# One load moved from the sync queue to GpSimd's queue in a cosine-similarity attention kernel, with new orders for the first pairs

## The chip, the cores and the metric

The kernel runs on one core of one Trainium2 chip. The metric is the device time of one execution in microseconds (us), taken as the median of several runs. Durations inside the kernel come from one further execution that was recorded by the hardware profiler; times inside it count from the start of its span. The engines are named as the profile names them: PE (TensorE), PEld (its weight load), DVE (VectorE), ACT (ScalarE), POOL (GpSimd) and SP (SyncE, which here only issues transfers). SPq, ACTq and POOLq are the instruction queues from which these engines issue DMAs.

## The reference

For each of 8 x 12 heads, Q, K and V are 512 x 64 in float32. The rows of Q and K are scaled to length one, their products are divided by tau = 0.1, a softmax runs over the keys, and the weights multiply V.

```python
Q_norm = Q / (np.linalg.norm(Q, axis=-1, keepdims=True) + 1e-10)
K_norm = K / (np.linalg.norm(K, axis=-1, keepdims=True) + 1e-10)
scores = np.einsum('bhqd,bhkd->bhqk', Q_norm, K_norm) / tau
weights = np.exp(scores - np.max(scores, axis=-1, keepdims=True))
weights = weights / (np.sum(weights, axis=-1, keepdims=True) + 1e-10)
return np.einsum('bhqk,bhkd->bhqd', weights, V).astype(np.float32)
```

## The kernel before

**Tiling.** Two heads of one batch make a *pair*; there are 48 pairs, numbered s = 0 to 47. A tensor of a pair is 256 KB and lies in SBUF as 128 partitions x 2 heads x 256 numbers. In the names below, w is 0 for Q and 1 for K, h is the head in the pair, and c counts four chunks of 128 keys.

**Operations of a pair**, with the names that the kernel gives them:

- LD(s,w) loads Q or K (L311; pair 0 is loaded by halves, one head each, at L308), LV(s) loads V (L314), ST(s) stores the output (L565).
- SQ(s,w) squares (L329 on ACT, L331 and L337 on POOL; pair 0: L239 on ACT, L241 on POOL). SSQ(s,w) lets PE add eight columns of the squares into one by matmuls with the identity (L354), and RED(s,w) sums what is left on DVE (L361; straight from the squares at L365).
- LOG and NEW(s,7) make the inverse norms of pairs 0 to 3 on ACT (L248, L252, L379, L382). From the fourth group of pairs on NEW is a chain of small DVE steps (L389, L390, L394, L398).
- SCL(s,w) multiplies by the inverse norms and rounds to bf16 (L420 on DVE or POOL, pair 0 at L258), TR(s,w) transposes on PE (L426; pair 0 at L266, L268) and EVA(s) copies the transposes of Q and K out of PSUM on DVE (L434; pair 0 at L279).
- SCO(s,c) makes the scores of a chunk on PE for both heads (L508), EXP(s,c) takes their exponential on ACT (L531; in pair 0 the first two chunks go head by head), VC(s) rounds V to bf16 on POOL (L536), PV(s,h,i) multiplies weights and V on PE (L548), and RCP and NRM divide by the row sums on DVE (L559, L561).

**What sets the order.** Nothing is decided at run time. Each engine has a fixed list of operation numbers, `ORDER` (L644), written out in the kernel, and executes it from front to back; a negative number is a filler matmul of that many columns. Before an operation the engine waits for the semaphores of the operations in its `needs`, so that a waiting operation also holds all that stands behind it in its list. Dependences are recorded by `Program.add` and turned into waits in `Program.run`. A DMA goes to the queue of the engine in whose list it stands and counts up a semaphore of its own buffer; loads of pairs 1 to 3 have one each (`first1_1` for K of pair 1).

**The first lists, in these names.** SP: LD(0,0) head 0, head 1, LD(1,0), LD(1,1), LD(2,0), LD(2,1), LV(0), LD(3,0), LD(3,1), LV(1) and so on. ACT issues the halves of LD(0,1), then: SQ(0,0) for both heads, LOG and NRMS of pair 0, SQ(1,0), a last NRMS, SQ(1,1) of head 0, SQ(2,0), EXP(0,1) of head 0, LOG(1), NEW(1), three more half EXPs of pair 0, LOG(2), EXP(0,2), NEW(2), EXP(0,3), EXP(1,0), LOG(3), EXP(1,1), NEW(3) and from there on EXP alone. POOL: four constants (`eps`, `one`, `eye`, `vone`), SQ(0,1) for both heads, SCL(0,1) for both heads, SQ(1,1) of head 1, SQ(2,1), VC(0), SQ(3,0), SQ(3,1), VC(1), SQ(4,0), SQ(5,0), VC(2), VC(3). PE: eight warm-up matmuls and fillers, TR(0,1) and TR(0,0) of head 0, a filler, SSQ(1,0), TR(0,1) of head 1, a filler, SCO(0,1) of head 0, SSQ(1,1), TR(0,0) of head 1, SCO(0,0) of head 0, and so on.

The ring of Q and K buffers is 15 pairs deep and that of V buffers 10 (`RINGS`, L622), so that none of the first loads waits for a buffer.

Of the kernel before, what the change touches and what calls it, by code (L numbers as in the profile page):

```python
# [108 lines left out]
def bass_cosine_similarity_attention_kernel(  # L109
# [15 lines left out]
    R_QK, R_V, R_SQ, R_QN, R_QT, R_ET, R_O, R_X = RINGS  # L125
# [31 lines left out]
    P = Program(nc)  # L157
# [19 lines left out]
    def key(name, s, *rest):  # L177
        return (name, s) + rest if s >= 0 else None
# [10 lines left out]
    def warm(e):  # L189
        for k in range(WARM):  # L190
            last = e.matmul(out=o_ps[1][:, :], lhsT=ident[:, :], rhs=warm_in[:, :], start=True, stop=True)
        return last
# [97 lines left out]
    def squares(s, w):  # L290
        return [("SQ", s, w if s in SQ_ON else 0)] + ([("SQ", s, w, 1)] if s in SQ_ON and isinstance(SQ_ON[s][w], tuple) else [])
# [5 lines left out]
    def pair(s):  # L297
# [6 lines left out]
        for w, x in ((0, Q), (1, K)):  # L304
            if s == 0:
                for h in range(2):
                    P.add(("LD", 0, w, h), "act" if w else "sp", "ldh", -1000 + h,  [],
                          lambda e, w=w, x=x, h=h: e.dma_start(out=qk[iq][:, w, h], in_=src(x, s)[:, h]), slot=f"head{w}_{h}")  # L308
                continue
            P.add(("LD", s, w), "sp", "ld1" if s == 1 else "ld", s, [*([("SCL", 0, w, 0), ("SCL", 0, w, 1), ("SQ", 0, w, 0), ("SQ", 0, w, 1)] if s == R_QK else [key("SCL", s - R_QK, w), *(squares(s - R_QK, w) if s >= R_QK else [])])],  # L310
                  lambda e, w=w, x=x: e.dma_start(out=qk[iq][:, w], in_=src(x, s)),  # L311
                  slot=f"first{s}_{w}" if s <= 3 else f"qk{iq}")
        P.add(("LV", s), "sp", "ld", s + VLAG, [key("VC", s - R_V)],
# [32 lines left out]
        for w in range(2):  # L346
# [16 lines left out]
            else:  # L363
                P.add(("RED", s, w), "dve", "red", due_red(s) + 0.5 * w, [*sqs, ("NRMS", 0, 0, 1), *new(g - R_X), *last_direct(s)],
                      lambda e, w=w, dst=dst: e.tensor_reduce(  # L365
                          out=dst, in_=sq[iqs][:, 8 * w : 8 * w + 8, :], axis=AX.X, op=ALU.add))
# [47 lines left out]
        for w in range(2):  # L414
# [5 lines left out]
                  lambda e, w=w, r=r: e.tensor_tensor(  # L420
                      out=qn[iqn][:, w].rearrange("p t h d -> p h t d"),
                      in0=qk[iq][:, w].rearrange("p h (t d) -> p h t d", t=NT), in1=r, op=ALU.mult))
# [199 lines left out]
RINGS = 15, 10, 6, 4, 4, 4, 8, 3  # L622
STORE_AT = 12
WARM = 8
START, PERIOD = 7.5, 3.62
M_SQ, M_NEW, M_SCL, M_VC = 5, 2, 2, 2
M_STEP = 0.23
# [12 lines left out]
def slack(s, most):  # L640
# [2 lines left out]

ORDER = {  # L644
# [10 lines left out]
    ),  # L655
    "pool": (
# [7 lines left out]
    ),  # L664
    "dve": (
# [24 lines left out]
    ),  # L690
# [79 lines left out]
```

## Time and profile before

| what | value |
|---|---|
| median of 3 runs | 189.69 us (189.34 to 190.37) |
| the profiled execution, its time | 189.78 us |
| the profiled execution, its span | 187.8 us |
| granted TensorE clock, mean | 0.995 |
| busy: ACT | 180.4 us, 96% of the span |
| busy: PE, DVE, POOL | 173.9, 173.0, 166.7 us |
| data moved | 50.76 MB, mean 270 GB/s |
| SPq issue of one 256 KB load of Q / K / V, median time to landing | 5.3 / 6.1 / 6.0 us |

The span is the time from the first instruction to the last; the execution's own time is 1.98 us longer. An engine's busy share is an average over the whole span. The chain that ended last is a path followed back from the last instruction, each piece to what released it; its share by engine tells what the end hangs on. In a timeline a row gives start, busy time, engine, line, operation, output tile <- input tile, shapes, count, and in brackets how long the engine had been idle before and which work ended that. Instructions of one engine overlap at their edges: an EXP of 128 x 1024 is busy for 1.18 us, but one follows the other every 0.92 us.

### The profile page before, as it was taken

How to read it: one execution, taken by the hardware profiler on the slowest of the kernel's cores; microseconds unless marked ns; L12 is line 12 of the kernel's file. 1: busy time of each engine (PE TensorE's matmuls, PEld its weight loads, DVE VectorE, ACT ScalarE, POOL GpSimd, SP SyncE). 2: the span in 40 equal slices, each digit the busy share in tenths (PEclk: the TensorE clock that was granted, in tenths of full speed). 3: DMA queues.
4: the chain of work that ended last, by engine and by line, in shares of the span. 5: the costliest groups of instructions: out<-in, count | busy, mean ns of one | idle time of the engine just before them, and what ended most of it. 6: DMA issues, size and time to landing. Idle time of an engine off the chain costs nothing.

```text
span 187.8 us, 6632 instructions
## 1 busy us (share of the span) xinstructions
PE 173.9 (93%) x2694; PEld 108.4 (58%) x2694; DVE 173.0 (92%) x546; ACT 180.4 (96%) x212; POOL 166.7 (89%) x152
## 2 busy tenths in 40 slices
PE   6799899999998999999999999999999889999993
PEld 2455566566565666666566666556655556655562
DVE  2688999999999999999999999999999999998873
ACT  4699999999999999999999999999999999999992
POOL 5499999999999999999999999999999999965600
PEclk9999999999999999999999999999999999999998
DMA  5999999899999998999999799995987722311333
GB/s 162 326 355 350 348 354 330 258 316 320 380 384 379 349 332 250 336 276 337 378 382 366 220 285 379 362 328 162 317 294 226 244 85 71 112 58 62 110 108 121
DMA packets 52446, 50.76 MB, mean 270 GB/s; under 512 B 3136, under 2 KB 52416, under 8 KB 52416
## 3 DMA queue, kind: packets, MB, share of 16 engines
q1 hardware_dynamic: 51984, 50.02, 80.7%
q8 instruction: 21, 0.34, 0.8%
q10 hardware_dynamic: 432, 0.33, 0.5%
q14 instruction: 9, 0.07, 0.1%
HBM read 37.75 MB, written 12.58 MB: 268 GB/s over the span
## 4 chain that ended last, share of the span: by engine, by line
ACT 93%; DMA 3%; SPq 1%; issue 1%; PE 1%; DVE 1%
ACT et L531 92%; DMA qk<-in_Q_dram 3%; PE ops L576 1%; SPq L311 0%; SPq L308 0%; DVE ob L589 0%; ACT sq L329 0%; ACT ys L379 0%; ACT nps L382 0%; DVE rd L587 0%; PE tps L576 0%
## 5 line engine op out<-in xcount | busy, mean ns | idle before, releaser
L531 ACT ACTIVATE et<-scps 128x1024 bf16<-128x1024 f32 (+1 forms) x191 | 174.1, 1170 | 0.0
L337 POOL TENSOR_TENSOR sq<-qk 128x1024 bf16<-128x1024 f32 x44 | 82.7, 1893 | 0.5 <-DMA qk<-in_K_dram 0.5
L508 PE MATMUL scps<-qt 64*128 64x512 bf16 x380 | 75.2, 386 | 7.3 <-ACT et L531 3.5
L548 PE MATMUL ops<-vb,et 128*128 128x65 bf16 x1504 | 73.4, 194 | 0.1
L548 PEld LDWEIGHTS ops<-vb,et 128*128 128x128 bf16 x1504 | 55.7, 98 | 28.7 <-issue 21.1
L561 DVE TENSOR_TENSOR ob<-ops,rd 128x256 f32<-128x256 f32 x94 | 38.7, 418 | 0.4
L420 DVE TENSOR_TENSOR qn<-qk,nps 128x512 bf16<-128x512 f32 x58 | 38.6, 676 | 0.5 <-ACT nps L382 0.5
L420 POOL TENSOR_TENSOR qn<-qk,rk 128x512 bf16<-128x512 f32 x36 | 37.5, 1054 | 1.0 <-DVE rk L394 0.9
L426 PE MATMUL tps<-ident,qn 128*128 128x128 bf16 x376 | 33.9, 221 | 0.4 <-POOL qn L420 0.2
L434 DVE COPY qt<-tps 128x1024 bf16<-128x1024 bf16 x47 | 32.2, 684 | 1.3 <-PE tps L426 0.9
L508 PEld LDWEIGHTS scps<-qt 64*128 64x128 bf16 x380 | 18.8, 92 | 24.9 <-ACT et L531 11.7
L365 DVE TENSOR_REDUCE nps<-sq 128x8 f32<-128x512 bf16 x48 | 32.5, 681 | 0.0
L536 POOL TENSOR_SCALAR vb<-vf 128x512 bf16<-128x512 f32 x48 | 30.3, 646 | 0.2
L426 PEld LDWEIGHTS tps<-ident,qn 128*128 128x128 bf16 x376 | 21.5, 98 | 12.8 <-issue 6.0
L354 PE MATMUL ops<-sq,ident 128*128 128x64 bf16 x368 | 18.4, 193 | 0.8 <-ACT nps L252 0.8
L559 DVE RECIPROCAL rd<-ops 128x4 f32<-128x4 f32 x94 | 16.1, 175 | 2.9 <-PE ops L548 2.2
L354 PEld LDWEIGHTS ops<-sq,ident 128*128 128x128 bf16 x368 | 13.7, 98 | 3.9 <-issue 2.0
L361 DVE TENSOR_REDUCE nps<-ops 128x8 f32<-128x64 f32 x40 | 8.7, 217 | 0.6 <-PE ops L354 0.4
L480 POOL TENSOR_TENSOR xz<-xz 128x1024 f32<-128x1024 f32 x2 | 3.8, 1892 | 3.3 <-DVE xz L475 3.3
L389 DVE TENSOR_TENSOR nps<-nps,ys 128x32 f32<-128x32 f32 (+1 forms) x30 | 6.2, 208 | 0.2
L390 DVE SCALAR_TENSOR_TENSOR nps<-nps,ys 128x32 f32<-128x32 f32 (+1 forms) x30 | 6.2, 208 | 0.0
L331 POOL TENSOR_TENSOR sq<-qk 128x512 bf16<-128x512 f32 (+1 forms) x4 | 3.7, 932 | 2.0 <-DMA qk<-in_K_dram 2.0
(61 smaller groups left out, 64.2 us busy)
## 6 DMA issues: line engine op xcount, KB each, us to landing
vf<-in_V_dram SPq DMA_DIRECT2D x48, 256.0 KB, 6.0
qk<-in_Q_dram SPq DMA_DIRECT2D x47, 256.0 KB, 5.3
qk<-in_K_dram SPq DMA_DIRECT2D x47, 256.0 KB, 6.1
out_dram<-ob SPq DMA_DIRECT2D x47, 256.0 KB, 4.2
qk<-in_Q_dram SPq DMA_DIRECT2D x2, 128.0 KB, 2.6
qk<-in_K_dram ACTq DMA_DIRECT2D x2, 128.0 KB, 2.8
out_dram<-ob SPq DMA_DIRECT2D x1, 128.0 KB, 1.7
out_dram<-ob ACTq DMA_DIRECT2D x1, 64.0 KB, 1.6
```

Of the source, the lines that this page charges most:

```text
L337: lambda e: e.tensor_tensor(out=sqf, in0=data, in1=data, op=ALU.mult))
L354: last = e.matmul(out=o_ps[bank][:, 320:384], lhsT=ident[:, :], rhs=sq[iqs][:, 8 * w : 8 * w + 8, 8 * k : 8 * k + 8], start=(k == 0), stop ...
L365: lambda e, w=w, dst=dst: e.tensor_reduce(out=dst, in_=sq[iqs][:, 8 * w : 8 * w + 8, :], axis=AX.X, op=ALU.add))
L420: lambda e, w=w, r=r: e.tensor_tensor(out=qn[iqn][:, w].rearrange("p t h d -> p h t d"), in0=qk[iq][:, w].rearrange("p h (t d) -> p h t d" ...
L426: last = e.transpose(t_ps[:, w, t, :], qn[iqn][:, w, t].rearrange("p h d -> p (h d)"), ident[:, :])
L434: lambda e: e.tensor_copy(out=qt[iqt][:, :, :, :].rearrange("p w t x -> p (w t x)"), in_=t_ps[:, :, :, :].rearrange("p w t x -> p (w t x)")))
L508: last = e.matmul(out=sc_ps[:, 2 * b + h, :], lhsT=qt[iqt][64 * h : 64 * h + 64, 1, c, :], rhs=qt[iqt][64 * h : 64 * h + 64, 0, :, :], sta ...
L531: lambda e, c=c, b=b, hs=hs: e.activation(out=et[iet][:, c, hs[0] : hs[-1] + 1, :], in_=sc_ps[:, 2 * b + hs[0] : 2 * b + hs[-1] + 1, :], f ...
L536: lambda e: e.tensor_scalar(out=vb[:, iq, :, :, 0:DIM].rearrange("p c h d -> p h c d"), in0=vf[iv][:, :, :].rearrange("p h (c d) -> p h c ...
L548: last = e.matmul(out=o_ps[h][:, 65 * t : 65 * t + 65], lhsT=et[iet][:, c, h, 128 * t : 128 * t + 128], rhs=vb[:, iq, c, h, :], start=(c = ...
L559: lambda e, h=h, grid=grid: e.reciprocal(out=rd[io][:, h, :], in_=grid[:, :, DIM]))
L561: lambda e, h=h, grid=grid: e.tensor_tensor(out=ob[io][:, h], in0=grid[:, :, 0:DIM], in1=rd[io][:, h, :].unsqueeze(2).to_broadcast([128, N ...
```

## The change

One operation changes its engine: LD(1,1), the load of pair 1's K, number 65, leaves SP's list and stands in POOL's list behind `vone` (number 4) and ahead of SQ(0,1) of head 0 (number 14). All loads behind it on SP move up one place. The lists of DVE, PE and POOL have another order up to about pair 14 (546 operations on DVE, of which the last 364 stand as before; 735 and 514 on PE; 148 and 96 on POOL). ACT's list is the same. No operation is added or removed and no dependence changes.

```diff
-            P.add(("LD", s, w), "sp", "ld1" if s == 1 else "ld", s, [...],
+            P.add(("LD", s, w), "pool" if (s, w) in LD_POOL else "sp", "ldp" if (s, w) in LD_POOL else "ld1" if s == 1 else "ld", s, [...],
                   lambda e, w=w, x=x: e.dma_start(out=qk[iq][:, w], in_=src(x, s)),
...
+LD_POOL = ((1, 1),)
...
     "sp": (
-        "7 8 64 65 103 104 11 141 142 66 179 180 105 222 223 143 256 257 181 298 299 224 332 333 258 375 376 300 "
+        "7 8 64 103 104 11 141 142 66 179 180 105 222 223 143 256 257 181 298 299 224 332 333 258 375 376 300 409 "
...
     "pool": (
-        "2 0 1 4 14 27 22 35 69 107 50 144 145 89 182 225 127 165 259 208 301 231 335 378 273 284 307 242 454 412 "
+        "2 0 1 4 65 14 27 22 35 69 107 50 144 145 89 182 127 225 165 259 208 301 231 284 242 335 378 273 412 307 "
...
     "dve": (
-        "5 13 15 26 28 19 24 21 32 37 71 73 34 109 78 111 76 80 116 114 147 149 118 152 154 183 156 185 226 228 "
+        "5 13 15 26 28 19 24 21 32 71 37 73 34 76 109 111 78 80 114 147 149 116 118 183 152 154 55 185 226 228 56 "
...
     "pe": (
-        "6 -256 -256 -256 -192 23 20 -256 70 36 -128 42 72 33 38 108 39 43 110 46 79 77 48 146 81 148 117 83 115 "
+        "6 -256 -256 -256 -192 23 20 -256 70 36 -128 42 72 33 38 108 39 43 110 77 46 48 79 146 148 81 83 57 115 "
```

In names, the pieces of the new lists that matter first:

- PE has the same list up to SSQ(2,1). Then it had SCO(0,2), TR(1,1), TR(1,0), SCO(0,3), SSQ(3,0), SCO(1,0), SSQ(3,1), TR(2,1), SCO(1,1); now it has TR(1,0), SCO(0,2), SCO(0,3), TR(1,1), SSQ(3,0), SSQ(3,1), SCO(1,0), SCO(1,1), PV(0,1,0), TR(2,0).
- DVE had SCL(1,1) ahead of SCL(1,0); now SCL(1,0) comes first, then RED(2,0), RED(2,1), SCL(1,1). RED(3,0) and RED(3,1) now stand between SCL(2,0) and SCL(2,1). EVA(3), which stood right behind RED(4,0), now stands behind SCL(3,0), SCL(3,1), RED(4,1), RED(5,0), RED(5,1), both RCP and NRM of pair 0 and the first four steps of NEW(4).
- POOL has VC(2) ahead of SQ(5,0), which was the other way round.

More of the change, by code (lines that the diff above doesn't have):

```diff
@@ L309, in pair @@
                 continue
-            P.add(("LD", s, w), "sp", "ld1" if s == 1 else "ld", s, [*([("SCL", 0, w, 0), ("SCL", 0, w, 1), ("SQ", 0, w, 0), ("SQ", 0, w, 1)] if s == R_QK else [key("SCL", s - R_QK, w), *(squares(s - R_QK, w) if s >= R_QK else [])])],
+            P.add(("LD", s, w), "pool" if (s, w) in LD_POOL else "sp", "ldp" if (s, w) in LD_POOL else "ld1" if s == 1 else "ld", s, [*([("SCL", 0, w, 0), ("SCL", 0, w, 1), ("SQ", 0, w, 0), ("SQ", 0, w, 1)] if s == R_QK else [key("SCL", s - R_QK, w), *(squares(s - R_QK, w) if s >= R_QK else [])])],
                   lambda e, w=w, x=x: e.dma_start(out=qk[iq][:, w], in_=src(x, s)),
```

81 rows, old and new, of the table ORDER are left out of this document.

## The prediction

> **What bounds the kernel now.** I read the page's busy shares first, then the chain that ended last, then the chain in order of time.
>
> ```profile
> PE 173.9 (93%) x2694; PEld 108.4 (58%) x2694; DVE 173.0 (92%) x546; ACT 180.4 (96%) x212; POOL 166.7 (89%) x152
> ACT 93%; DMA 3%; SPq 1%; issue 1%; PE 1%; DVE 1%
> ```
>
> ```profile
> 2.67 5.60 DMA qk<-in_Q_dram
> ...
> 8.29 0.63 ACT sq L329
> ...
> 15.53 167.90 ACT et L531 x183
> ```
>
> The end hangs on ACT's exponentials: from 15.53 to 183.43 they stand back to back, 167.90 / 183 = 0.917 us each, with nothing waited for. ACT's whole idle time is 187.8 - 180.4 = 7.4 us, and it lies at the two ends. No re-ordering of other engines can win anything after 8.29, because ACT waits for nothing there; it can only lose. What can be won lies before 8.29, where the chain runs through a load: LD(2,0), issued at 2.67, landed 5.60 later. So I looked at ACT alone over the first 9 us.
>
> ```profile
> 6.85 0.63 ACT L329 ACTIVATE sq<-qk 128x512 bf16<-128x512 f32 x1 [1.01 <-DMA qk<-in_Q_dram]
> 7.39 0.16 ACT L252 ACTIVATE nps<-ys 128x4 f32<-128x4 f32 x1
> 7.61 0.42 ACT L329 ACTIVATE sq<-qk 128x256 bf16<-128x256 f32 x1
> 8.29 0.63 ACT L329 ACTIVATE sq<-qk 128x512 bf16<-128x512 f32 x1 [0.27 <-DMA qk<-in_Q_dram]
> 8.83 0.58 ACT L531 ACTIVATE et<-scps 128x512 bf16<-128x512 f32 x1
> ```
>
> ACT waits 1.01 us for Q of pair 1 (SQ(1,0) at 6.85), then for Q of pair 2 another 0.27. Between them, SQ(1,1) at 7.61 reads K of pair 1, the load that is moved; the DMA view gives it 5.4 us from its issue at 2.16, so that it landed at about 7.6, just in time. Three loads bound the start, in this order: LD(1,0), LD(1,1), LD(2,0).
>
> **The move of the load.** These are SP's two issues around it and POOL's first work:
>
> ```profile
> 2.16 0.47 SPq L311 DMA_DIRECT2D qk<-in_K_dram  x1
> 2.67 0.47 SPq L311 DMA_DIRECT2D qk<-in_Q_dram  x1
> ```
>
> ```profile
> 1.33 0.63 POOL L186 MEMSET vb<- 128x120 bf16 x1
> 3.56 1.26 POOL L241 TENSOR_TENSOR sq<-qk 128x256 bf16<-128x256 f32 x2 [1.59 <-DMA qk<-in_K_dram]
> ...
> 7.65 0.61 POOL L331 TENSOR_TENSOR sq<-qk 128x256 bf16<-128x256 f32 x1 [1.12 <-DMA qk<-in_K_dram]
> 9.10 1.04 POOL L331 TENSOR_TENSOR sq<-qk 128x512 bf16<-128x512 f32 x1 [0.84 <-DMA qk<-in_K_dram]
> ...
> 10.81 2.04 POOL L331 TENSOR_TENSOR sq<-qk 128x512 bf16<-128x512 f32 x2
> ```
>
> *Removed from SP:* one issue, 2.67 - 2.16 = 0.51 us. LD(2,0), LD(2,1), LV(0) and all later loads are issued 0.51 earlier. *Added to POOL:* one issue behind `vone`, at 1.96, against 2.16 before. No POOL issue is in this trace. Its cost on POOL lies between SP's own 0.47 and, above, two passes of POOL's widest row, 2 x 1.89 = 3.8 (L337). I take 1 to 1.9, since it has 256 rows of 1 KB to describe and POOL does a 128x1024 operation in 1.89. POOL is idle from 1.96 to 3.56 (the 1.59 in the row), and behind it SQ(0,1), SCL(0,1) and the transposes of pair 0 have another 0.76: PE idles that long before SSQ(1,0) (7.54 in PE's timeline), which hangs on LD(1,0). So up to 1.59 + 0.76 = 2.35 us of POOL's time cost nothing; without that cover all of it would fall on pair 0's chain.
>
> What the transfers then do is the real question, and the windows answer it in part:
>
> ```profile
> 3.00:4.00 1.00, 1.00 (x4) 0.33 (x3) 0.23 (x1) 0.42 (x1) 0.45 (x1) 1.00 0.95 264
> 4.00:5.00 1.00, 1.00 (x4) 0.42 (x3) 0.99 (x4) 0.73 (x3) 0.78 (x2) 1.00 0.68 213
> 5.00:6.00 1.00, 0.61 (x6) 0.30 (x4) 0.69 (x2) 0.76 (x4) 0.69 (x2) 1.00 0.90 294
> 8.00:9.00 1.00, 1.00 (x18) 0.60 (x14) 0.73 (x4) 0.73 (x3) 0.26 (x1) 1.00 1.10 380
> ```
>
> The last two numbers of a row are the DMA engines' share and GB/s. From 8 us on they move 380 GB/s; from 3 to 6 they are 0.95, 0.68 and 0.90 busy, so (0.05 + 0.32 + 0.10) = 0.47 us of all 16 engines is unused. A second queue may fill it: 0.47 x 380 GB/s is 179 KB of K's 256. *Gain end:* LD(2,0) lands 0.51 earlier, at 7.77. Then ACT's 0.27 gap closes, but SCO(0,1) runs from 8.16 for 0.39 behind SSQ(1,0), and EXP(0,1) can't start before about 8.57 instead of 8.83. The next step, LOG(1) at 9.31, needs RED(1,1), which ended at 9.14 (8.66 with 0.48 for two); so 0.17 to 0.27 is won, no more, while LD(1,0) still lands at 6.84. *Loss end:* K's 256 KB take turns with LD(1,0) instead of standing behind it. At 380 GB/s they are 0.69 us; Q then lands up to 0.69 later and SQ(1,0), SSQ(1,0) and SCO(0,1) with it. EXP(0,1) starts at 8.16 + 0.69 + 0.41 = 9.26 instead of 8.83: 0.43 lost, and LOG(1), 0.17 after what it needs, about 0.5. Since the same three loads still have to be moved before SQ(2,0) and the landing that counts is the last engine's, I take a third of Q's possible delay: +0.2, within -0.27 to +0.5.
>
> The Trainium skill, "DMA: Bandwidth & Descriptors", section "Queues, rings and completion order", says that each DMA engine goes round its queues packet by packet; the trace agrees that queues share, as the 128 KB halves from SP and ACT, issued together, landed after 2.5 to 2.9 us each. By that rule alone the loss end would hold wherever K's packets are ready before Q's are through.
>
> **The new orders.** Up to SSQ(2,1) on PE nothing moves. Two places are tight. *SSQ(3,1) ahead of SCO(1,0):* EXP(0,3) and EXP(1,0) are the row "12.39, 1.95 x2", so EXP(1,0) starts near 13.35 and SCO(1,0) must start by 13.35 - 0.39 = 12.96. SSQ(3,1) needs SQ(3,1), which ends on POOL at 10.81 + 2.04 = 12.85; SSQ holds PE for 0.27 (13.06 to 13.33), so SCO(1,0) would start at about 13.17: 0.2 late. It was ahead of SSQ(3,1) before. Where POOL's chain, which starts from LD(2,1) at 9.10 after 0.84 idle, comes 0.51 earlier, this is nothing. *EVA(3):* SCO(3,0) was done at 20.18 for an EXP at about 20.98. By the pitches in DVE's timeline (0.62 for SCL, EVA and the wide RED, 0.13 for small ones, 0.33 for NRM) the new list puts EVA(3) at 20.1 to 20.8 where it was at 17.40, since RED(5,0) now follows SQ(5,0), which stands 0.6 later behind VC(2). SCO(3,0) would end at 21.15, 0.17 late, or in time with earlier loads. These stalls don't add where ACT has shifted already. I take +0.1, between 0 and 0.4. The cover of every other moved operation is ACT's own queue of exponentials.
>
> **Sum.** 189.78 (the profiled execution: 187.8 of span and 1.98 around it; the median of the runs is 189.69, 0.09 lower) + 0.2 + 0.1 = 190.08, rounded down to the median's side: 190.0. Its own range is -0.27 to +0.9 about 189.7: 189.4 to 190.6.
>
> **Rivals.**
>
> *Slower: K of pair 1 comes late.* Place: SQ(1,1) on ACT at 7.61 and its other half on POOL at 7.65. It decides once K lands after 7.61 + 0.27 = 7.9; from there each us costs one. If POOL's issue takes the upper bound 3.8, SQ(0,1) starts at 5.76 instead of 3.56; less the 0.76, 1.4 late: 191.2. If K's first bytes come 1.5 later than SP would have brought them, it lands at 9.1: 190.9 to 191. For it: no row shows this queue, and the loads behind it on SP took 5.4 to 6.5 to land. Against: it is issued 0.2 earlier than on SP, POOL is idle there, and a load of twice the halves' size that starts at 2 has 5.6 us.
>
> The Trainium skill, "DMA: Bandwidth & Descriptors", section "SWDGE vs HWDGE vs iDMA", says that a DMA from GpSimd has its descriptors computed in software there and those of SP and ACT come from hardware. That speaks for this rival; no run here shows it yet, and DVE and POOL are idle until 3.56.
>
> *Faster: Q of pair 1 comes early.* If K behind it on the same queue was what kept LD(1,0) and LD(2,0) from landing, the 1.01 gap closes too: 189.78 - 1.01 - 0.1 = 188.7. For it: the unused 0.47 us. Against: LD(1,0) stood ahead of K on SP's queue already, and it can't be held by what is behind it.
>
> *Slower by the orders:* if sharing moves LD(2,1) back by a load's 0.69, SQ(3,1) ends at 13.54, SCO(1,0) starts at 13.9 instead of 12.96, and ACT stops for 0.9: 190.7, with 0.2 from the start 190.9. It decides once SQ(3,1) ends after 12.65. Against: POOL's row shows 0.84 idle before SQ(2,1), all of it the load's.
>
> *The move does nothing* (K lands when it did, Q too): 189.8, inside the forecast.
>
> **How the numbers follow.** What the runs of this kernel can tell from no change is about 0.5%, 0.95 us: 188.74 to 190.64. The forecast (with the move that does nothing) has 0.60, K late 0.20, Q early 0.11, the orders 0.09. Faster: the 0.11. Slower: 0.18 of K late, 0.06 of the orders, 0.02 of the forecast's upper edge: 0.26. Same: the rest, 0.63. The range leaves out the far half of Q early and the upper third of K late: 188.9 to 191.3.
>
> **What would show it.** SQ(1,0) on ACT starts at 6.85 to 7.2, SQ(1,1) by 8.1, the first EXP at 8.6 to 9.3; POOL's issue ends before 4.3 and SQ(0,1) follows K's landing as before. EXP(1,0) and EXP(3,0) have at most 0.2 us of idle before them. The rival with K late shows ACT idle before SQ(1,1), the one with Q early shows SQ(1,0) near 6, that of the orders an ACT gap before EXP(1,0). ACT idle in the middle of the run, or exponentials not 0.917 apart, would prove the frame wrong.

## The result, and the profile after

| | before | after |
|---|---|---|
| median of 20 runs each, interleaved | 189.22 us (from 188.79) | 189.96 us (from 189.58) |
| ratio, with its 95% interval | 1 | 1.0041 (1.0028 to 1.0053) |
| the profiled execution, its span | 187.8 us | 188.1 us |

The changed kernel is slower by 0.41%, 0.74 us by the medians of all runs. That is less than the 0.5% called no change in the prediction, but the interval excludes a ratio of 1. Three of the 20 runs of the changed kernel took 192.8 to 193.0 us at a lower granted clock (0.98); the ratio leaves them out, and without them its median is 189.92, 0.70 above before. The two profiled executions differ by only 0.3 us; the reason is found below.

First the busy shares of the page of after, then its chain in order of time (start, duration, what), then ACT's and POOL's first work in the timeline.

```profile
PE 174.3 (93%) x2694; PEld 108.7 (58%) x2694; DVE 173.0 (92%) x546; ACT 180.5 (96%) x212; POOL 167.1 (89%) x153
```

```profile
1.70 5.48 DMA qk<-in_Q_dram
7.20 0.63 ACT sq L329
...
7.91 0.39 PE ops L354 x8
...
8.57 0.33 PE scps L508
...
15.78 167.94 ACT et L531 x183
```

```profile
7.20 0.63 ACT L329 ACTIVATE sq<-qk 128x512 bf16<-128x512 f32 x1 [1.09 <-DMA qk<-in_Q_dram]
...
7.83 0.92 ACT L329 ACTIVATE sq<-qk 128x256 bf16<-128x256 f32 x2
8.93 0.60 ACT L531 ACTIVATE et<-scps 128x512 bf16<-128x512 f32 x1 [0.18 <-PE scps L508]
```

```profile
1.55 0.91 POOL L311 DMA_DIRECT2D qk<-in_K_dram  x1
3.60 0.61 POOL L241 TENSOR_TENSOR sq<-qk 128x256 bf16<-128x256 f32 x1 [1.13 <-DMA qk<-in_K_dram]
...
6.78 0.61 POOL L331 TENSOR_TENSOR sq<-qk 128x256 bf16<-128x256 f32 x1
```

The same 183 exponentials stand back to back for 167.94 us (167.90 before); they start at 15.78 instead of 15.53, and the span is longer by as much. So the time went before that point. The chain now hangs on LD(1,0), the load of Q of pair 1, instead of LD(2,0): SQ(1,0) starts at 7.20 instead of 6.85, and behind it SSQ(1,0) and SCO(0,1) on PE hold the first exponential, which waited 0.18 for them. ACT does the two operations at 7.83 (SQ(1,1) and SQ(2,0), merged in one row under the first one's shape) with no wait: both of their loads are there. POOL's issue took 0.91 us, inside its idle time, and POOL does its half of SQ(1,1) at 6.78 instead of 7.65: K came in time, Q came late.

### The profile page after: what moved, and what is told of

The parts are those of the page before. It is cut to its first block, busy times and chain, and to the rows that moved or that the text cites. A ratio compares the mean times of both kernels' runs of the same rounds, so it can differ in the third digit from the quotient of the medians.

```text
span 188.1 us, 6636 instructions
## 1 busy us (share of the span) xinstructions
PE 174.3 (93%) x2694; PEld 108.7 (58%) x2694; DVE 173.0 (92%) x546; ACT 180.5 (96%) x212; POOL 167.1 (89%) x153
## 4 chain that ended last, share of the span: by engine, by line
ACT 93%; DMA 3%; PE 1%; issue 1%; DVE 1%; SPq 0%
ACT et L531 92%; DMA qk<-in_Q_dram 3%; PE ops L576 1%; SPq L308 0%; DVE ob L589 0%; ACT sq L329 0%; ACT ys L379 0%; ACT nps L382 0%; PE ops L354 0%; PE scps L508 0%; DVE rd L587 0%; PE scps L266 0%; ACT nps L252 0%; PE tps L576 0%; PE scps L194 0%
## 5 line engine op out<-in xcount | busy, mean ns | idle before, releaser
L191 PE MATMUL ops<-warm_in,ident 128*128 128x512 bf16 x8 | 3.6, 631 | 1.4 <-POOL ident L181 1.4
```

## The experiments

Ratios are against runs of the kernel before on the same chip in the same session. This table puts the profiles of all runs side by side. "Q1" is the load of Q of pair 1, with the times at which it had landed by the trace's semaphore events on 12 of the 16 DMA engines and on all; "K1" and "Q2" likewise, on all. The stream goes from the start of the first exponential to that of the last but one. Each row's times are those of one profiled execution, and the runs were made on several chips, so that single landings compare only roughly.

| run | K1 issued by | Q1 on 12 | Q1 | K1 | Q2 | first EXP | stream | span | ratio (95%) |
|---|---|---|---|---|---|---|---|---|---|
| before | SP | 5.79 | 6.83 | 7.58 | 8.27 | 8.83 | 174.64 | 187.8 | 1 |
| e3, before again | SP | 5.45 | 6.04 | 6.99 | 7.71 | 8.27 | 174.64 | 187.2 | 0.9999 (0.9983 to 1.0015) |
| e2, orders alone | SP | 5.61 | 5.67 | 6.59 | 7.32 | 8.11 | 175.22 | 187.7 | 1.0033 (1.0017 to 1.0049) |
| e5, old POOL list | SP | 4.81 | 5.68 | 6.56 | 7.46 | 8.15 | 174.94 | 187.4 | 1.0019 (1.0003 to 1.0034) |
| e6, new POOL list | SP | 5.43 | 6.07 | 6.79 | 7.51 | 8.07 | 175.09 | 187.5 | 1.0026 (1.0009 to 1.0043) |
| after | POOL | 6.96 | 7.18 | 6.71 | 7.89 | 8.93 | 174.83 | 188.1 | 1.0041 (1.0028 to 1.0053) |
| e10, after again | POOL | 6.35 | 7.06 | 6.64 | 7.83 | 8.81 | 174.85 | 188.0 | 1.0042 (1.0018 to 1.0066) |
| e1, move alone | POOL | 6.57 | 6.80 | 6.78 | 7.50 | 8.55 | 174.87 | 187.8 | 1.0023 (1.0009 to 1.0038) |
| e4, K1 on ACT's queue | ACT | 5.70 | 6.58 | 7.51 | 7.82 | 8.37 | 174.89 | 187.6 | 1.0023 (1.0004 to 1.0042) |
| e7, before, more ACT work | SP | 5.32 | 5.46 | 6.60 | 8.42 | 9.50 | 174.65 | 188.5 | 1.0012 (0.9995 to 1.0029) |
| e8, e2, more ACT work | SP | 5.04 | 5.64 | 6.37 | 7.11 | 8.19 | 174.84 | 187.4 | 1.0023 (1.0006 to 1.0040) |
| e9, K1 late on POOL | POOL | 5.76 | 6.26 | 11.44 | 6.93 | 12.31 | 177.36 | 194.0 | 1.0338 (1.0313 to 1.0363) |
| e11, SQ(2,0) on POOL | SP | 5.53 | 6.89 | 7.53 | 8.30 | 8.64 | 175.02 | 188.0 | 1.0008 (0.9993 to 1.0023) |

**e1: the move alone.** The lists of before, with number 65 moved.

```diff
+LD_POOL = ((1, 1),)
     "sp": (
-        "7 8 64 65 103 104 11 141 142 66 179 180 105 222 223 143 ...
+        "7 8 64 103 104 11 141 142 66 179 180 105 222 223 143 ...
     "pool": (
-        "2 0 1 4 14 27 22 35 ...
+        "2 0 1 4 65 14 27 22 35 ...
```

> The lists of the kernel before, with LD(1,1) alone moved to POOL's queue. Theory (sharing): K of pair 1 takes turns with Q of pair 1 on the DMA engines, so Q lands later and the exponentials start later; the move alone then carries the whole loss: ratio 1.003 to 1.005, SQ(1,0) on ACT at 7.1 to 7.3 instead of 6.85, the stretch of back-to-back exponentials starts 0.25 to 0.5 later. Rival (orders): the new lists cost it; then this run is level with before, 0.999 to 1.001, and SQ(1,0) may be late but the gap is made up before EXP(1,0). Rival (issue on POOL delays pair 0): SQ(0,1) of head 1 ends 0.3 later on POOL, and the chain through pair 0 rather than Q of pair 1 holds the first EXP; ratio as in the theory, but the idle time before SQ(1,0) is under 0.5.

These are two rows of ACT in this run:

```profile
6.83 0.63 ACT L329 ACTIVATE sq<-qk 128x512 bf16<-128x512 f32 x1 [0.85 <-DMA qk<-in_Q_dram]
...
8.55 0.60 ACT L531 ACTIVATE et<-scps 128x512 bf16<-128x512 f32 x1 [0.18 <-PE scps L508]
```

Measured 1.0023 (1.0009 to 1.0038): the move costs by itself, less than the theory had. SQ(1,0) started at 6.83, earlier than expected for the theory and no later than in the first profile of before (6.85); it is late against the second profile of before (6.06, below). The chain of this run too goes through LD(1,0) and PE. Pair 0 was not what held: ACT idled 0.85 before SQ(1,0). Against its own rival (the orders alone cost, a ratio up to 1.001) the theory holds, as the interval reaches that rival only with its edge; whether the move is the whole, this run can't say.

**e2: the orders alone.** The new lists of DVE, PE and POOL, number 65 back on SP behind 64.

```diff
     "sp": (
-        "7 8 64 103 104 ...
+        "7 8 64 65 103 104 ...
     "pool": (
-        "2 0 1 4 65 14 27 ...
+        "2 0 1 4 14 27 ...
```

> The new lists of DVE, PE and POOL, with LD(1,1) back on SP between LD(1,0) and LD(2,0). Theory (sharing): level with before within 0.1% (0.999 to 1.001), or up to 0.1% slower by SSQ(3,1) ahead of SCO(1,0): an ACT gap of at most 0.2 us before EXP(1,0). Rival (orders): 1.003 to 1.005, with ACT idle before EXP(1,0) or EXP(3,0) summing to 0.5 us or more.

Measured 1.0033 (1.0017 to 1.0049): the orders cost by themselves, so the theory that they are free fell. The first EXP was early here (8.11), and the stream was long: 175.22 against 174.64. The place is not one of the two that the prediction named. PE's timeline of this run shows it, and POOL's:

```profile
29.71 0.40 PE L426 MATMUL tps<-ident,qn 128*128 128x128 bf16 x4 [0.56 <-POOL qn L420]
```

```profile
18.43 1.90 POOL L337 TENSOR_TENSOR sq<-qk 128x1024 bf16<-128x1024 f32 x1 [0.87 <-DMA qk<-in_K_dram]
...
23.73 1.22 POOL L536 TENSOR_SCALAR vb<-vf 128x512 bf16<-128x512 f32 x2
24.91 3.75 POOL L337 TENSOR_TENSOR sq<-qk 128x1024 bf16<-128x1024 f32 x2
28.61 1.05 POOL L420 TENSOR_TENSOR qn<-qk,rk 128x512 bf16<-128x512 f32 x1
```

TR(6,1) stood on PE, and all behind it, until POOL had done SCL(6,1) at 29.66. The row of two at 23.73 is VC(6) and VC(5), 1.2 us, which the new list has ahead of SQ(8,0), SQ(9,0) and SCL(6,1); before, both stood behind SCL(6,1). The row at 18.43 shows a second condition: POOL had idled 0.87 for K of pair 6, which landed 8.5 us after its issue, against 6.9 to 7.4 in nine others and 7.9 and 8.1 in e9 and e11. PE had got to TR(6,1) at 29.15 (29.71 less 0.56). By an estimate from these rows SCL(6,1) would have ended at 28.8 without the late load, and at 28.5 without the two VC ahead of it: the stall took both.

**e3: the kernel before, again.**

> The kernel before, unchanged, for a second profile: its first one took 189.78 us, 0.56 over the median of its runs. If the landing of Q of pair 1 is what differs from one execution to the next, a profile nearer to the median shows SQ(1,0) earlier than 6.85, at about 6.3, and the exponentials starting earlier by as much. If SQ(1,0) is again at 6.8 to 6.9, the difference lies elsewhere (in the middle of the run or around the span). Ratio 0.999 to 1.001 in any case.

This is ACT's start in the second profile of before:

```profile
6.06 0.63 ACT L329 ACTIVATE sq<-qk 128x512 bf16<-128x512 f32 x1
...
7.73 0.63 ACT L329 ACTIVATE sq<-qk 128x512 bf16<-128x512 f32 x1 [0.31 <-DMA qk<-in_Q_dram]
8.27 0.58 ACT L531 ACTIVATE et<-scps 128x512 bf16<-128x512 f32 x1
```

Measured 0.9999 (0.9983 to 1.0015), as expected. No wait before SQ(1,0): Q1 had landed on all engines at 6.04 against 6.83 in the first profile. The first EXP is 0.56 earlier, the stream is the same to 0.01, and the span is 0.6 shorter. The execution that the prediction was worked out from was one with a late Q1.

**e4: K1 on ACT's queue.** ACT's queue instead of POOL's; the only other edit keeps ACT's own wait for the load.

```diff
-            P.add(("LD", s, w), "sp", ...
+            P.add(("LD", s, w), "act" if (s, w) in LD_ACT else "sp", ...
+LD_ACT = ((1, 1),)
     "act": (
-        "9 10 3 12 25 ...
+        "9 10 65 3 12 25 ...
```

> The lists of the kernel before, with LD(1,1) issued from ACT's queue right behind the two halves of K of pair 0, ahead of the table load; SQ(1,1) on ACT keeps its wait for it. ACT pays one issue of about 0.47 us before the table load, which ended 0.33 before Q of pair 0 landed, so up to 0.15 of it shows. Theory (sharing): a second queue of any kind lets K take turns with Q of pair 1, so SQ(1,0) is as late as with POOL's queue or later (7.1 to 7.5): ratio 1.003 to 1.006. Rival (POOL's software queue): without GpSimd in it Q lands as before or earlier, and LD(2,0) too: ratio 0.997 to 1.001.

Measured 1.0023 (1.0004 to 1.0042): between the range of the theory and that of the rival, with an interval that reaches into both, so that the ratio decides neither. SQ(1,0) started at 6.60, not at the 7.1 to 7.5 of the theory, and Q1 had landed on 12 engines at 5.70, as with SP; K1 came at 7.51, later than with POOL. ACT's own issue made the table load start 0.49 later, but the second Square of pair 0 waited 0.22 for its load again, so that by then this was made up. The queues did share: this is the DMA view of the window 4.4 to 5.6 us, by queue (packets, MB, share of 16 engines).

```profile
q1 hardware_dynamic: 161, 0.15, 48.8%
q10 hardware_dynamic: 178, 0.18, 44.2%
```

q1 is SP's queue, with Q1 in it, and q10 ACT's, with K1 alone in it. A second queue of either kind takes a share; with ACT's, Q1 suffered less in this profile.

**e5 and e6: which list.** e5 has the new lists of PE and DVE with POOL's list of before, e6 POOL's new list with the rest as before; LD(1,1) is on SP in both.

```diff
     "pool": (
-        "... 471 361 318 488 530 ...
+        "... (e5: the whole list of before; e6: the whole list of after without 65)
```

> The new lists of PE and DVE with POOL's list of before, LD(1,1) on SP. In the run of the new orders alone, TR(6,1) held PE for 0.56 us until POOL had done SCL(6,1) at 29.66; VC(6) and VC(5), 1.2 us together, now stand ahead of SQ(8,0), SQ(9,0) and SCL(6,1). Theory (POOL's list is the fault): with the old POOL list the exponentials run through from first to last in 174.6 to 174.8 us as in the kernel before, no PE idle before TR(6,1), ratio 0.998 to 1.001. Rival (the lists of PE and DVE are the fault, POOL is only where it shows): ratio 1.002 to 1.004, with a gap between exponentials of 0.4 us or more in all.

> The counterpart: POOL's new list alone, the lists of PE, DVE and SP as before. Theory (POOL's list is the fault): SCL(6,1) ends about 1 us later than in the kernel before (28.7 there), PE waits for it before TR(6,1), and EXP(5,3) and EXP(6,0) come 0.4 to 0.7 late: ratio 1.002 to 1.004. Rival (PE and DVE lists): 0.999 to 1.001.

e6 gave 1.0026 (1.0009 to 1.0043), and the same stall at the same place:

```profile
29.62 0.40 PE L426 MATMUL tps<-ident,qn 128*128 128x128 bf16 x4 [0.56 <-POOL qn L420]
```

So of the lists POOL's new one is enough for this stall; the PE and DVE lists are those of before. Here too POOL had waited, 0.62, for K of pair 6, which again took 8.5 us to land; why it was late in these two runs is not known. e5 lost the stall, but gave 1.0019 (1.0003 to 1.0034), between what the two theories expected: the new lists of PE and DVE cost something too. Its stream is 0.30 longer than before's, 0.15 of it by the fourth exponential (from 8.15 to 10.18, 2.04, against 1.88 in e3). With these intervals neither theory can be called the whole.

**e7 and e8: more work on ACT ahead of the first EXP.** One Square more, into a tile that nothing reads; e7 on the kernel before, e8 on e2.

```diff
+    spin = sb("spin", [128, 512], bf16)
-                        emit = lambda e, half=half, dst=dst: e.activation(out=dst, in_=half, func=ACT.Square)
+                        emit = lambda e, half=half, dst=dst, n=s == 2: [e.activation(out=o, in_=half, func=ACT.Square) for o in ([spin[:, :]] if n else []) + [dst]][-1]
```

> The kernel before with one more Square of Q of pair 2 on ACT, into a tile that nothing reads, right ahead of SQ(2,0): the first exponential comes 0.55 later and nothing else changes. Theory (before has no other floor, so that a late start is paid in full): ratio 1.0025 to 1.0035, start of the exponentials and end both 0.5 to 0.6 later. Rival (the start is not what the time hangs on): under 1.001.

> The new orders alone (LD(1,1) on SP) with the same additional Square on ACT. Theory (the new POOL list sets a floor of about 31.6 us for EXP(6,0), so a start up to 0.5 later is hidden behind it): the ratio to before stays where the new orders alone had it, 1.003 to 1.004, and the gap before EXP(6,0) shrinks from 0.5 to under 0.15. Rival (the two costs add): 1.006 to 1.007.

e7 gave 1.0012 (0.9995 to 1.0029), less than expected for 0.55 us, with an interval that reaches both ranges; part of the Square may be covered by the wait for SCO(0,1), which isn't shown. Where the start was late (9.50 in its profile, with Q2 landed at 8.42), the span paid all of it: 1.23 later than e3 at the first EXP, 1.3 at the end. e8 gave 1.0023 against 1.0033 without the Square: it did not add up, as the theory had it, and the stall before TR(6,1) was gone. But its EXP(6,0) came at 31.3 where the theory had a floor of 31.6. The floor is not fixed: POOL's SQ(6,0) had waited 0.87 for K of pair 6 in e2 (the row at 18.43), and waited for nothing in e8, where that K landed at 16.82 instead of 18.35. The first EXP of e8 was only 0.08 later than that of e2 (8.19 against 8.11), so that in this profile the timely load took the stall away and not a late start. Since e7 itself fell short, these two runs don't settle how much of the stall a late start hides.

**e9: K1 late on POOL.** As e1, with number 65 behind both SQ(0,1).

```diff
     "pool": (
-        "2 0 1 4 65 14 27 22 35 ...
+        "2 0 1 4 14 27 65 22 35 ...
```

> The move alone (lists of before) with LD(1,1) two places further back in POOL's list, behind both SQ(0,1): its packets then start about 2.1 us after an issue near 4.8, at 6.9, when Q of pair 1 is through. Theory (K's packets take Q's turns on the DMA engines): Q of pair 1 has landed on half of the engines by 4.7 to 5.1, as in every run with K on SP, against 6.0 and 6.1 with K issued at 1.55 on POOL. K itself lands at 8 to 9, SQ(1,1) waits for it and the first EXP starts at 8.9 to 9.8: ratio 1.004 to 1.008. Rival (the queue of GpSimd slows Q whenever it is used, or Q's landing varies by chance): half of the engines at 5.5 or later.

ACT's and POOL's timeline of this run:

```profile
11.46 0.93 ACT L329 ACTIVATE sq<-qk 128x256 bf16<-128x256 f32 x2 [4.49 <-DMA qk<-in_K_dram]
```

```profile
4.90 0.91 POOL L311 DMA_DIRECT2D qk<-in_K_dram  x1
```

Q1 had landed on half of the engines at 5.43, between what the theory and the rival expected; on 12 at 5.76 and on all at 6.26, in the range of the runs with K1 on SP (4.81 to 5.79, 5.46 to 6.89). With K1 out of its way Q1 is not late on the last engines, and Q2, issued 0.51 earlier as in the changed kernel, landed at 6.93, earlier than in any other run. The price was far off: K1's first packet started 4.1 us after the issue, at 9.04, and ACT waited 4.49 for it: 1.0338 (1.0313 to 1.0363), where 1.004 to 1.008 was expected.

**e10: the changed kernel again.**

> The changed kernel once more, for a second profile. Theory (sharing): Q of pair 1 lands on half of the engines at 5.8 to 6.2 again and on the last at 6.6 to 7.3; the first EXP at 8.5 to 9.0, against 8.1 to 8.3 in most profiles with K on SP. The exponentials then take 174.8 from first to last, 0.2 more than in the kernel before, of which 0.15 lies before the fourth. Rival (one unlucky execution): half of the engines by 5.1, first EXP by 8.3. Ratio 1.003 to 1.005 in both.

1.0042 (1.0018 to 1.0066). First EXP 8.81, Q1 on all engines 7.06, stream 174.85 with 2.03 to the fourth exponential, as the theory had it. One of its marks failed: half of the engines had Q1 at 4.88, as with SP. It is the last engines that tell: on 12 engines Q1 lands at 6.35 to 6.96 in the three runs with K1 issued early on POOL, and never later than 5.79 in the others.

**e11: a try at a faster kernel.** All loads on SP, SQ(2,0) on POOL.

```diff
-SQ_ON = {1: ("act", ("act", "pool")), 2: ("act", "pool"), 3: ("pool", "pool")}
+SQ_ON = {1: ("act", ("act", "pool")), 2: ("pool", "pool"), 3: ("pool", "pool")}
```

> A try at a faster kernel, from the kernel before with all loads on SP: SQ(2,0) goes from ACT to POOL, ahead of SQ(2,1). ACT loses 0.54 us of work ahead of the first EXP, which can then start when SCO(0,1) is done, 0.3 to 0.4 earlier; POOL gains 1.04, of which about 0.8 lies in its wait for K of pair 2. If ACT's start is what the time hangs on: ratio 0.998 to 0.9995. If POOL's later chain (SQ(3,1), then SCL(6,1)) shows on ACT: 1.000 to 1.003.

1.0008 (0.9993 to 1.0023): no gain shown. ACT had the time, and waited for PE's SCO(0,1) instead, 0.67 us in this profile, where Q1 was late. No run here beat the kernel before.

## Why the prediction was right, and where its sizes were off

**The frame held.** ACT's exponentials bound the kernel and the change could act only ahead of them and by stalls. The forecast of no change by its 0.5% held (1.0041), and the median of 189.96 is the predicted 190.0, partly by luck: the sum started from an execution of before with a late Q1 (189.78, where the median of 20 is 189.22). The change itself was put at +0.3 and measured +0.70 to +0.74. That the moved load would share the DMA engines with LD(1,0) was right, and the new orders were right only in kind; these terms were mis-sized:

**LD(1,0) taking turns with K1 (put at +0.2, within -0.27 to +0.5).** The step that failed is "I take a third of Q's possible delay". Q1 lands on all engines at 7.18, 7.06 and 6.80 with K1 early on POOL (mean 7.01), and at 6.83, 6.04, 5.67, 5.68, 6.07, 5.46, 5.64 and 6.89 with K1 on SP (mean 6.04): 1.0 later, where the possible delay was put at 0.69. The first EXP starts at 8.55 to 8.93 (mean 8.76) against 8.07 to 8.83 (mean 8.29, in the five runs with the same work on ACT): 0.47 later. That is the whole of the prediction's loss end (0.43 to 0.5) and not a third of it; the rest of Q1's delay is hidden, since with an early Q1 the next wait is that for Q2 (0.31 in e3). Single executions overlap, but the packets of the trace don't: SP's queue had moved its first 512 packets of 1024 bytes, as many as pair 0's Q and Q1 have, by 5.64 to 5.81 in the three runs with K1 early on POOL, by 5.25 in e4 and by 4.43 to 5.07 in the nine others. The DMA view, by queue, shows the sharing: first the changed kernel in the window 4.4 to 5.6 us, then e3.

```profile
q0 software_dynamic: 50, 0.17, 49.6%
q1 hardware_dynamic: 147, 0.14, 48.7%
```

```profile
q1 hardware_dynamic: 328, 0.32, 87.1%
```

q0 is POOL's queue, with K1 alone in it, and q1 is SP's. Together they move 0.31 MB, as SP's alone did (0.32 here, 0.27 in the first profile of before): little was filled in, and SP's queue, with Q1 in it, was left with 0.14. The prediction had read 0.47 us of unused engines at 380 GB/s into its windows, but in these the engines were 0.95 busy at 264 GB/s and 0.90 busy at 294: busy engines moved less there. That also ends the **gain end**: LD(2,0) was issued 0.51 earlier and landed at 7.50 to 7.89, where SP alone brings it at 7.11 to 8.42.

The Trainium skill ("DMA: Bandwidth & Descriptors", "Queues, rings and completion order") says that each DMA engine goes round the queues that have work, a packet at a time. The trace agrees that the queues share. What the prediction had not considered is the size: POOL's 64 data packets have 4096 bytes each, SP's 1024. In these 1.2 us POOL's queue moved more than SP's (0.17, 0.22 and 0.19 MB against 0.14, 0.10 and 0.14 in after, e10 and e1), and in e4 ACT's, with packets as short as SP's, moved 0.18 against 0.15. That the longer packets win the share is likely, but not shown: no run changed the size of the packets alone, and 50 packets to 147 in the window is not turn for turn.

**The new orders (put at +0.1, 0 to 0.4).** Alone they cost 0.33% (0.17 to 0.49), 0.6 us by the ratio. The two places named did nothing in the changed kernel: EXP(1,0) followed EXP(0,3) without a gap, as POOL's chain was earlier (SQ(3,1) ended at 12.49), and EVA(3) ran at 19.98 to 20.66, near the 20.1 to 20.8 worked out, without a gap before EXP(3,0). What the working missed is SCL(6,1) behind VC(6) and VC(5) on POOL, ten microseconds further on: shown in e2 and e6, where a late K of pair 6 added to it. In the changed kernel that stall doesn't appear: SCL(6,1) ends at 29.58, and PE comes to TR(6,1) only at 29.89. Two reasons are possible and not separated: ACT is later by the late Q1, and PE with it; and K of pair 6 came in time (17.68, 7.3 us after its issue). In e8's profile it was the load.

The ratios of the two parts, 0.23% and 0.33%, sum to 0.56% where the whole is 0.41%; with these intervals the runs can't tell whether they add, and the 0.18% between e1 and the changed kernel is no larger than they are wide. By the profiles the first EXP is 0.5 to 0.7 later in after and e10 than in e3 and the stream 0.2 longer, together 0.7 to 0.9 where 0.70 to 0.74 was measured. The 0.2 needn't come from the orders: e1, with the lists of before, has the same stream (174.87) and the same 2.03 to the fourth exponential. So no cost of the orders is seen in the changed kernel's profiles, and that their +0.1 brought the sum nearer is luck.

**POOL's issue (put at 1 to 1.9, covered).** It took 0.91 us, and nothing waited for it.

**The rivals.** *K late* did not occur: K1 landed at 6.64 to 6.78, no later than on SP (6.37 to 7.58); e9 shows how dear it would have been. *Q early* is refuted by the landings above. *Slower by the orders* was right in kind for the orders alone (e2) and wrong in place. *The move does nothing* is refuted by e1 (1.0009 to 1.0038).

## What to carry to other kernels

A load moved to another queue doesn't only leave its old place: it can become a competitor of the load that was ahead of it, as here, where it took 0.17 to 0.22 MB in the time in which that load's queue got 0.10 to 0.14. So ask which of the loads the bounding engine needs first, and keep the others behind it on the same queue. Read the start of a run from several executions: the landing on the last DMA engine varied by 1.4 us between kernels whose early loads were the same, more than the change moved. And new lists of orders must be checked far behind the start, with a load that comes a microsecond late there (here K of pair 6 on POOL), before they are judged by the first stalls.

## What the runs showed of the hardware that was not expected

- A 256 KB load from POOL's queue goes in 64 packets of 4096 bytes; the same load from SP goes in 256 of 1024. While both had work, from 9.2 to 10.0 us in e9, POOL's queue moved 0.20 MB and SP's 0.11.
- From POOL's issue to its first packet it took 2.1 to 2.6 us at the start of a run (1.55 to 3.70, 3.80 and 4.12) and 4.1 us in the one run that issued it later, with SP's queue at work (4.90 to 9.04); SP's first load took 1.0 (0.79 to 1.80).
- The last of the 16 DMA engines can lag far behind the rest: in the first profile of before Q1 had landed on eight at 4.81 and on the last at 6.83.
